# Pairing the small fp32 products of a recurrence on different rows of TensorE, with causal selects on GpSimd

## The chip, the cores and the metric

The kernel runs on one NeuronCore of a Trainium2 chip. The metric is the device time of one execution in microseconds (us). Its engines are TensorE (PE in the profile; its weight loads PEld), VectorE (DVE), ScalarE (ACT), GpSimd (POOL) and SyncE (SP, which here issues DMAs). Each works through its own instructions in program order.

## The reference, cut to what matters

A two-layer trunk over 256 positions of width 2048. Layer 0 projects its normalized input once and feeds two mixers, a gated MLP (A) and an RWKV-7 recurrence (B) with 16 heads of 64; their outputs go through one output projection. Layer 1 is attention; each layer ends in a SwiGLU FFN. The change touches only B:

```python
kk = kk / jnp.maximum(jnp.sqrt(jnp.sum(kk * kk, axis=-1, keepdims=True)), 1e-12)
...
def step(state, inp):
    r_t, w_t, k_t, v_t, a_t, b_t = inp
    sa = jnp.einsum('bhij,bhj->bhi', state, a_t)
    state = (state * w_t[:, :, None, :] + sa[..., None] * b_t[:, :, None, :]
             + v_t[..., None] * k_t[:, :, None, :])
    y_t = jnp.einsum('bhij,bhj->bhi', state, r_t)
    return state, y_t
...
y = ((y - mean) * lax.rsqrt(var + B_GN_EPS)).reshape(bsz, s, B_WIDTH)
...
y = (y + bonus.reshape(bsz, s, B_WIDTH)) * g.astype(f32)
```

## The kernel before, in words

The dense projections are the main stream. In `dense32` (layer 0's input projections) a chunk of 512 KB of fp32 weights is loaded by SP and multiplied in four fp32 matmuls of 128x512 (L901). Every fp32 matmul is two passes in the trace, so a chunk is eight L901 records. In `dense` (everything after) a chunk is split into a high part (L191 on ACT) and a low part (L192 on DVE) and takes twelve single-pass matmuls (L203 to L205).

The recurrence is a generator, `rk_gen`. After each chunk `pump` runs the adaLN work (an `ada` chunk of 512 KB and one DVE dot product, L117) and then lets `rk_gen` go on until a credit is spent: each `yield x` costs x, each chunk gives 1.8 to 3. So the small products stand between the chunks of the main stream in each engine's queue; inside that, the program's scheduler orders instructions by when their operands and PSUM banks come free. The small products share a pool of four PSUM banks (`msbank`).

The recurrence in chunks of 64 positions, with its lines: decay and `a` gates from two low-rank products (L511); the norm of kk, spread back over a head's 64 channels by `head_bcast` (L474, a 16-row product); the masked 64x128 products of every head (L637), whose results go to `SCN` (mask product L640 on DVE) and `SRA` (half by L643 on ACT and a mask product L644 on POOL, half by L647 on DVE); the inverse of a unit triangular matrix per head and chunk, by 32x32 transposes (L665), a chain of 31 pairs of DVE products (L672, L674), transposes back (L680, L683) and two 32x32 matmuls that merge the halves (L690, L699); then the state steps c = 0 to 3, with `x_free` (L738), L815, L831, L845, L852 and L862; the bonus and gate (`gate_bonus`, L474 on `bon`, L759); and a group norm in two parts (L779 to L798, L474 on the rows in `SRA`). Layer 0's output projection follows (`YA`, then `YB`).

Heads 2g and 2g+1 lie on rows 0 to 63 and 64 to 127 of a tile (index e). TensorE has 128 rows and 128 columns of cells; a product of 64, 32 or 16 rows uses only those rows.

## Time and profile before

| | |
|---|---|
| median of 3 runs | 2560.14 us (2558.58 to 2572.45) |
| the profiled execution's own time | 2557.72 us |
| its span (first to last instruction) | 2555.7 us, 2.0 us less |
| PE busy | 2429.3 us (95%) |
| DVE busy | 1619.6 us (63%) |
| ACT busy | 1037.1 us (41%) |
| POOL busy | 102.0 us (4%) |
| mean granted TensorE clock | 0.978 of full speed |

PE's records overlap (a matmul's record lasts longer than the distance to the next one), so PE's rate is read from the distance between starts. Times in the rows count from the start of the span. The recurrence runs from about 150 to 535 us.

### The profile page before, as it was taken

To read this page: it belongs to the slowest core of one execution; us is meant where nothing else is said; L and a number is where in the kernel's file an instruction comes from. 1 tells how busy PE (TensorE), PEld (TensorE's weight loads), DVE (VectorE), ACT (ScalarE), POOL (GpSimd) and SP (SyncE) were. 2 spreads that over 40 slices of the span, in tenths; PEclk is the share of its full clock that TensorE was granted. 3 is DMA by queue.
4 is the path that set the end of the run, shared out by engine and by line. 5 is a ranking of instruction groups with operands and counts; after the bars stand their busy time and mean duration, and the time that the engine had idled before them with its cause. 6 is when DMAs were issued, how large, how long until landed. Compare 5 with 4: busy or idle time off the path is not lost. (4 is left out here: it accounts for less than half of the span.)

```text
span 2555.7 us, 29570 instructions
## 1 busy us (share of the span) xinstructions
PE 2429.3 (95%) x10944; PEld 1860.5 (73%) x10944; DVE 1619.6 (63%) x2176; ACT 1037.1 (41%) x1423; POOL 102.0 (4%) x83
## 2 busy tenths in 40 slices
PE   4998989998999999999998999999899999999998
PEld 2443537677887777888887777778778888888886
DVE  5656794568877777654446778865776455444444
ACT  1042103347443443444445444446544444444443
POOL 0002210001000000000001001100100000000000
PEclk8998999899999999999999999999999999999999
DMA  9987776574988888755554888855587555556554
GB/s 377 417 302 242 259 245 212 177 265 146 329 317 306 317 296 310 234 205 191 193 193 146 302 292 311 300 196 206 201 318 265 188 190 189 189 190 206 191 194 151
DMA packets 166528, 623.47 MB, mean 244 GB/s; under 512 B 18560, under 2 KB 18752, under 8 KB 161392
## 3 DMA queue, kind: packets, MB, share of 16 engines
q1 hardware_dynamic: 164288, 612.74, 68.7%
q10 hardware_dynamic: 2096, 8.86, 0.9%
q8 instruction: 85, 1.39, 0.2%
q14 instruction: 59, 0.48, 0.1%
HBM read 619.39 MB, written 2.13 MB: 243 GB/s over the span
## 5 line engine op out<-in xcount | busy, mean ns | idle before, releaser
L192 DVE TENSOR_TENSOR wl<-w,wh 128x1024 fp32r<-128x1024 f32 x688 | 836.8, 1223 | 532.9 <-ACT wh L191 531.7
L191 ACT ACTIVATE wh<-w 128x1024 fp32r<-128x1024 f32 x688 | 728.3, 1059 | 1005.4 <-PE mm L205 941.7
L117 DVE SCALAR_TENSOR_TENSOR ada<-ada,cond 128x1024 f32<-128x1024 f32 x320 | 392.9, 1229 | 286.1 <-DMA ada<-in_w_ada_dram 285.2
L204 PE MATMUL mm<-wl,hF 128*128 128x512 f32 x1408 | 552.4, 392 | 15.0 <-DVE wl L192 14.8
L203 PE MATMUL mm<-wh,hF 128*128 128x512 f32 x1408 | 552.9, 393 | 0.0
L205 PE MATMUL mm<-wh,hFl 128*128 128x512 f32 x1408 | 549.9, 391 | 0.0
L204 PEld LDWEIGHTS mm<-wl,hF 128*128 128x128 f32 x1408 | 264.5, 188 | 81.8 <-DVE wl L192 28.6
L205 PEld LDWEIGHTS mm<-wh,hFl 128*128 128x128 f32 x1408 | 264.4, 188 | 54.5
L203 PEld LDWEIGHTS mm<-wh,hF 128*128 128x128 f32 x1408 | 264.5, 188 | 53.7
L204 PE MATMUL mm<-wl,aH 128*128 128x512 f32 x704 | 276.9, 393 | 0.0
L205 PE MATMUL mm<-wh,aL 128*128 128x512 f32 x704 | 275.5, 391 | 0.0
L203 PE MATMUL mm<-wh,aH 128*128 128x512 f32 x704 | 274.6, 390 | 0.0
L901 PE MATMUL mm<-w,xT 128*128 128x512 f32 x448 | 216.3, 630 | 4.6 <-DMA w<-in_w_in_dram 4.6
L901 PEld LDWEIGHTS mm<-w,xT 128*128 128x128 f32 x448 | 86.2, 201 | 105.9 <-issue 97.7
L203 PE MATMUL mm<-wh,hA 128*128 128x512 f32 x384 | 155.7, 405 | 0.0
L204 PE MATMUL mm<-wl,hA 128*128 128x512 f32 x384 | 152.3, 397 | 3.1 <-DVE wl L192 3.1
L203 PEld LDWEIGHTS mm<-wh,aH 128*128 128x128 f32 x704 | 132.2, 188 | 30.1
L204 PEld LDWEIGHTS mm<-wl,aH 128*128 128x128 f32 x704 | 132.3, 188 | 28.6
L205 PEld LDWEIGHTS mm<-wh,aL 128*128 128x128 f32 x704 | 132.3, 188 | 27.7
L205 PE MATMUL mm<-wh,hAl 128*128 128x512 f32 x384 | 150.8, 393 | 0.0
L204 PEld LDWEIGHTS mm<-wl,hA 128*128 128x128 f32 x384 | 72.8, 190 | 20.1 <-DVE wl L192 6.3
L205 PEld LDWEIGHTS mm<-wh,hAl 128*128 128x128 f32 x384 | 72.7, 189 | 15.1
(312 smaller groups left out, 2049.5 us busy)
## 6 DMA issues: line engine op xcount, KB each, us to landing
w<-in_w_ffn_in_dram SPq DMA_DIRECT2D x352, 512.0 KB, 3.9
ada<-in_w_ada_dram SPq DMA_DIRECT2D x320, 512.0 KB, 5.1
w<-in_w_ffn_out_dram SPq DMA_DIRECT2D x176, 512.0 KB, 3.6
w<-in_w_qkv_dram SPq DMA_DIRECT2D x96, 512.0 KB, 5.2
w<-in_w_in_dram SPq DMA_DIRECT2D x56, 512.0 KB, 5.2
w<-in_w_out_dram SPq DMA_DIRECT2D x32, 512.0 KB, 3.8
w<-in_w_o_dram SPq DMA_DIRECT2D x32, 512.0 KB, 3.3
KB<-in_w_ada_dram SPq DMA_DIRECT2D x12, 1024.0 KB, 12.0
```

Source lines behind the costliest of these rows:

```text
L117: V.scalar_tensor_tensor(w, w, 1.0, cond[:, k0:k0 + n], op0=OP.mult, op1=OP.mult, accum_out=dst)
L191: A.activation(wh[:, :, :ncol], w32[:, :, :ncol], AF.Copy)
L192: V.tensor_sub(wl[:, :, :ncol], w32[:, :, :ncol], wh[:, :, :ncol].bitcast(F32))
L203: T.matmul(o, h, wh[:, k, :ncol], start=(kt == 0), stop=False)
L204: T.matmul(o, h, wl[:, k, :ncol], start=False, stop=False)
L205: T.matmul(o, l, wh[:, k, :ncol], start=False, stop=(kt == nkt - 1))
L901: T.matmul(ps[t], xT[:, kt, tsl(t)], w[:, k, :], start=(kt == 0), stop=(kt == KT - 1))
```

## The change

Products that use 64, 32 or 16 rows are issued alternately on two groups of rows, each into a PSUM bank of its own: the two low-rank products (now 64 rows each instead of one 128-row product against zeros), `head_bcast` (a copy of the 16 rows is kept on rows 32 to 47, `twice`), the masked products over e, the merge of block b with the second half of the merge of block b-2, the state products over e, and L831 with the next chunk's `x_free`. `SRA` is evicted by ACT alone and masked by eight `affine_select` on POOL. The yields change from 8x0.7 to 4x1.0 (low-rank products), from 16x0.5 to 8x1.0 (masked products) and from 8x0.6 to 6x1.0 (merges).

```diff
-    indT = x0i[0:16, :].rearrange("h (g p) -> h g p", g=8)
+    indT = [x0i[32 * q:32 * q + 16, :].rearrange("h (g p) -> h g p", g=8) for q in range(2)]
...
-    A.dma_start(indT, io["indT"])
-
-    def head_bcast(out, g, rows):
-
-        T.matmul(out, indT[:, g, :], rows, start=True, stop=True)
+    for q in range(2):
+        A.dma_start(indT[q], io["indT"])
+
+    def twice(rows):
+
+        A.activation(rows[32:48], rows[0:16], AF.Copy)
+
+    def head_bcast(g0, n, rows):
+
+
+        w = rows.free_size()
+        ps = [msbank()[:, :n // 2 * w].rearrange("p (g s) -> p g s", g=n // 2) for _ in range(2)]
+        for i in range(n // 2):
+            for q in range(2):
+                T.matmul(ps[q][:, i, :], indT[q][:, g0 + 2 * i + q, :], rows[32 * q:32 * q + 16],
+                         start=True, stop=True)
+        return ps
...
-        for which, dst, bias in ((0, E[:, 0], "w0"), (1, AT, "a0")):
-            for g2 in range(4):
-                ps = msbank()
-                psv = ps.rearrange("p (g s) -> p g s", g=2)
+        for g2 in range(4):
+            psv = [msbank().rearrange("p (g s) -> p g s", g=2) for _ in range(2)]
+            for i in range(2):
+                g = 2 * g2 + i
+                for x in range(2):
+                    xs = slice(64 * x, 64 * x + 64)
+                    T.matmul(psv[x][:, i, :], w2a2[xs, g * P:(g + 1) * P], tz[xs],
+                             start=True, stop=True)
+            for x, dst, bias in ((0, E[:, 0], "w0"), (1, AT, "a0")):
                 for i in range(2):
                     g = 2 * g2 + i
-                    T.matmul(psv[:, i, :], w2a2[:, g * P:(g + 1) * P], tz[:, which, :],
-                             start=True, stop=True)
-                for i in range(2):
-                    g = 2 * g2 + i
-                    A.activation(dst[:, g, :], psv[:, i, :], AF.Sigmoid, bias=col(bias, g))
-                yield 0.7
+                    A.activation(dst[:, g, :], psv[x][:, i, :], AF.Sigmoid, bias=col(bias, g))
+            yield 1.0
...
+        rn2 = SCf[0:48, 0:S]
+        rn = rn2[0:16]
         A.activation(rn, pn[:16, :S], AF.Sqrt)
         V.tensor_scalar(rn, rn, 1e-12, None, op0=OP.max)
         V.reciprocal(rn, rn)
+        twice(rn2)
         yield 2.3
-        for g2 in range(4):
-            ps = msbank()
-            psv = ps.rearrange("p (g s) -> p g s", g=2)
-            for i in range(2):
-                head_bcast(psv[:, i, :], 2 * g2 + i, rn)
-            V.tensor_mul(Kk[:, 2 * g2:2 * g2 + 2, :], Kk[:, 2 * g2:2 * g2 + 2, :], psv)
-            yield 0.6
+        for g0 in (0, 4):
+            ps = head_bcast(g0, 4, rn2)
+            for q in range(2):
+                gs = slice(g0 + q, g0 + 4, 2)
+                V.tensor_mul(Kk[:, gs, :], Kk[:, gs, :], ps[q])
+            yield 1.2
...
-        ne = 0
         for c in range(4):
             cs = slice(c * 64, (c + 1) * 64)
-            for e in range(2):
-                es = slice(64 * e, 64 * e + 64)
-                for hf in range(2):
-                    ps = msbank()
-                    psv = ps.rearrange("p (g x t) -> p g x t", g=4, x=2)
-                    for i in range(4):
-                        g = 4 * hf + i
-                        T.matmul(psv[:, i], KB[es, g, c].rearrange("p b t -> p (b t)"),
+            for hf in range(2):
+                ps = [msbank().rearrange("p (g x t) -> p g x t", g=4, x=2) for _ in range(2)]
+                for i in range(4):
+                    g = 4 * hf + i
+                    for e in range(2):
+                        es = slice(64 * e, 64 * e + 64)
+                        T.matmul(ps[e][:, i], KB[es, g, c].rearrange("p b t -> p (b t)"),
                                  RA[es, :, g, cs], start=True, stop=True)
-                    gs = slice(4 * hf, 4 * hf + 4)
-                    V.tensor_tensor(SCv[:, c, gs, e, :], psv[:, :, 1, :],
+                gs = slice(4 * hf, 4 * hf + 4)
+                for e in range(2):
+                    V.tensor_tensor(SCv[:, c, gs, e, :], ps[e][:, :, 1, :],
                                     mk[:, 1:2, :].to_broadcast([P, 4, 64]), op=OP.mult)
-                    if ne % 2 == 0:
-                        A.activation(SRv[:, c, gs, e, :], psv[:, :, 0, :], AF.Copy)
-                        G.tensor_tensor(SRv[:, c, gs, e, :], SRv[:, c, gs, e, :],
-                                        mk[:, 0:1, :].to_broadcast([P, 4, 64]), op=OP.mult)
-                    else:
-                        V.tensor_tensor(SRv[:, c, gs, e, :], psv[:, :, 0, :],
-                                        mk[:, 0:1, :].to_broadcast([P, 4, 64]), op=OP.mult)
-                    ne += 1
-                    yield 0.5
+                    A.activation(SRv[:, c, gs, e, :], ps[e][:, :, 0, :], AF.Copy)
+                yield 1.0
+            for x in range(2):
+                sr = SRA[64 * x:64 * x + 64, 16 * c:16 * c + 16, :]
+                G.affine_select(sr, sr, pattern=[[0, 16], [1, 64]], compare_op=OP.is_ge, fill=0.0,
+                                base=0, channel_multiplier=-1)
...
-        for b in range(4):
-            ps = msbank()
+        def merge_ops(b, second, ps):
             for i in range(16):
                 n = 16 * b + i
-                T.matmul(ps[96:128, i * 32:(i + 1) * 32], SCN[64:96, n, 32:64], T0[64:96, n, :],
-                         start=True, stop=True)
-            A.activation(T0[96:128, 16 * b:16 * b + 16, :],
-                         ps[96:128, :].rearrange("p (n j) -> p n j", n=16), AF.Copy)
-            yield 0.6
...
+                if second:
+                    yield (ps[64:96, i * 32:(i + 1) * 32], T0[96:128, n, :], SCN[96:128, n, 32:64])
+                else:
+                    yield (ps[96:128, i * 32:(i + 1) * 32], SCN[64:96, n, 32:64], T0[64:96, n, :])
+
+        for st in range(6):
+            job = [(b, x) for b, x in ((st, 0), (st - 2, 1)) if 0 <= b < 4]
+            banks = [msbank() for _ in job]
+            for ops in zip(*(merge_ops(b, x, ps) for (b, x), ps in zip(job, banks))):
+                for o, l, r in ops:
+                    T.matmul(o, l, r, start=True, stop=True)
+            for (b, x), ps in zip(job, banks):
+                dst, o = (SCN[64:96, 16 * b:16 * b + 16, 32:64], 64) if x else (
+                    T0[96:128, 16 * b:16 * b + 16, :], 96)
+                A.activation(dst, ps[o:o + 32, :].rearrange("p (n j) -> p n j", n=16), AF.Copy)
+            yield 1.0
...
-        def x_free(c):
-            px = [msbank() for _ in range(2)]
+        def x_free(c, px):
             for e in range(2):
                 for g in range(8):
                     h = 2 * g + e
-                    T.matmul(px[e][64:128, g * 64:(g + 1) * 64], SCN[0:64, c * 16 + h, :],
-                             VU2[0:64, c % 2, h, :], start=(g == 0), stop=(c == 0 and g == 7))
-            return px
+                    yield (px[e][64:128, g * 64:(g + 1) * 64], SCN[0:64, c * 16 + h, :],
+                           VU2[0:64, c % 2, h, :], g == 0, c == 0 and g == 7)
+
+        def mm_list(ops):
+            for o, l, r, st, sp in ops:
+                T.matmul(o, l, r, start=st, stop=sp)
...
-            pb = msbank()
-            pbv = pb.rearrange("p (g s) -> p g s", g=2)
-            for i in range(2):
-                head_bcast(pbv[:, i, :], 2 * g2 + i, bon)
-            V.tensor_tensor(VT[:, gs, :], VT[:, gs, :], pbv, op=OP.mult)
+            for q, pb in enumerate(head_bcast(2 * g2, 2, bon)):
+                g = 2 * g2 + q
+                V.tensor_tensor(VT[:, g:g + 1, :], VT[:, g:g + 1, :], pb, op=OP.mult)
...
-            for e in range(2):
-                es = slice(64 * e, 64 * e + 64)
-                if c:
-                    for g in range(8):
+            if c:
+                for g in range(8):
+                    for e in range(2):
+                        es = slice(64 * e, 64 * e + 64)
                         T.matmul(px[e][64:128, g * 64:(g + 1) * 64], RA[es, 1, g, cs],
                                  Sst[es, g, :], start=False, stop=(g == 7))
+            for e in range(2):
...
+            pu = [msbank() for _ in range(2)]
+            if c < 3:
+                px = [msbank() for _ in range(2)]
+                nx = x_free(c + 1, px)
             for b in range(2):
-                ps = msbank()
                 for i in range(8):
                     h = 8 * b + i
-                    T.matmul(ps[64:128, i * 64:(i + 1) * 64], SCN[64:128, c * 16 + h, :],
+                    T.matmul(pu[b][64:128, i * 64:(i + 1) * 64], SCN[64:128, c * 16 + h, :],
                              X0[64:128, h, :], start=True, stop=True)
+                    if c < 3:
+                        mm_list([next(nx)])
                 A.activation(VU[64:128, 8 * b:8 * b + 8, :],
-                             ps[64:128, :].rearrange("p (h i) -> p h i", h=8), AF.Copy)
-            if c < 3:
-                px = x_free(c + 1)
```

Three places on PE show what moves. First the merge of the triangular blocks (`AT` and `SCN` are its operands, L690 its first product, L699 its second; L901 is a main-stream chunk). Before:

```order
L901 MATMUL mm<-w_1444,xT 128x512 x4
L690 MATMUL ms<-AT,SCN 32x32 x48
L901 MATMUL mm<-w_1507,xT 128x512 x4
L690 MATMUL ms<-AT,SCN 32x32 x16
L699 MATMUL ms<-SCN,AT 32x32 x32
```

Now (L709 is both products, L917 the chunk):

```order
L917 MATMUL mm<-w_1437,xT 128x512 x4
L709 MATMUL ms<-AT,SCN 32x32 x32
L917 MATMUL mm<-w_1482,xT 128x512 x4
L709 MATMUL ms<-AT,SCN 32x32
L709 MATMUL ms<-SCN,AT 32x32
```

The third block's first products, which stood ahead of a chunk, stand behind it and alternate with second products. Next the state step c = 1 (L831 is the inverse times X0, L738 is `x_free` of the next chunk). Before:

```order
L831 MATMUL ms<-x0i,SCN 64x64 x8
L901 MATMUL mm<-w_1873,xT 128x512
L831 MATMUL ms<-x0i,SCN 64x64 x8
L738 MATMUL ms<-AT,SCN 64x64 x4
L901 MATMUL mm<-w_1873,xT 128x512
L738 MATMUL ms<-AT,SCN 64x64 x12
```

Now (L847 and L753):

```order
L847 MATMUL ms<-x0i,SCN 64x64 x8
L917 MATMUL mm<-w_1875,xT 128x512
L753 MATMUL ms<-AT,SCN 64x64 x4
L847 MATMUL ms<-x0i,SCN 64x64 x8
L917 MATMUL mm<-w_1875,xT 128x512
L753 MATMUL ms<-AT,SCN 64x64 x12
```

Here the two products are not alternated; four `x_free` products moved ahead of the second eight. Last the bonus (L474, now L484) and the gate (L759, now L770). Before:

```order
L474 MATMUL ms<-bon,x0i 128x256 x2
L759 MATMUL ms<-sg,SRA 128x256 x4
L901 MATMUL mm<-w_2111,xT 128x512 x3
L474 MATMUL ms<-bon,x0i 128x256 x2
L759 MATMUL ms<-sg,SRA 128x256 x4
```

Now:

```order
L484 MATMUL ms<-bon,x0i 128x256 x2
L917 MATMUL mm<-w_2115,xT 128x512
L770 MATMUL ms<-sg,SRA 128x256 x4
L917 MATMUL mm<-w_2115,xT 128x512
L484 MATMUL ms<-bon,x0i 128x256
L917 MATMUL mm<-w_2178,xT 128x512
L484 MATMUL ms<-bon,x0i 128x256
L917 MATMUL mm<-w_2178,xT 128x512
```

Only the first pair of bonus products stands together; the two of each later pair are parted by a chunk's matmul.

## Rows read from the trace of the kernel before

**Rows 1.** The page: busy time of each engine, and the granted TensorE clock in 40 equal slices of the span (tenths).

```profile
PE 2429.3 (95%) x10944; PEld 1860.5 (73%) x10944; DVE 1619.6 (63%) x2176; ACT 1037.1 (41%) x1423; POOL 102.0 (4%) x83
...
PEclk8998999899999999999999999999999999999999
```

**Rows 2.** Busy time by stretch: stretch and its length, then PE, PEld, DVE, ACT, POOL busy (instructions), granted clock, share of DMA, GB/s.

```profile
140.00:302.65 162.65, 152.97 (x480) 74.20 (x479) 104.28 (x207) 51.14 (x96) 28.17 (x29) 0.96 0.77 262
302.65:387.15 84.50, 70.74 (x240) 34.43 (x239) 77.48 (x133) 8.15 (x14) 15.11 (x8) 0.91 0.69 230
387.15:541.00 153.85, 153.48 (x1293) 106.47 (x1294) 89.17 (x153) 56.87 (x91) 0.00 (x0) 0.93 0.63 209
468.00:485.00 17.00, 17.00 (x32) 7.47 (x32) 7.44 (x13) 4.33 (x8) 0.00 (x0) 0.50 0.39 125
```

**Rows 3.** Timeline of PE: start, length, line, shape, count; the low-rank products, a chunk, and `head_bcast` of the kk norm.

```profile
158.47 2.75 PE L511 MATMUL ms<-tz,w2a 128*128 128x256 f32 x12
161.06 3.60 PE L901 MATMUL mm<-w,xT 128*128 128x512 f32 x8
...
212.48 2.85 PE L474 MATMUL ms<-SCN,x0i 16*128 16x256 f32 x12
...
220.59 1.12 PE L474 MATMUL ms<-SCN,x0i 16*128 16x256 f32 x4
```

**Rows 4.** Timeline of PE: the masked products among the chunks (in brackets idle time before, and who ended it).

```profile
279.79 1.16 PE L637 MATMUL ms<-RA,KB 64*128 64x128 f32 x8
280.88 3.70 PE L901 MATMUL mm<-w,xT 128*128 128x512 f32 x8
284.51 3.16 PE L637 MATMUL ms<-RA,KB 64*128 64x128 f32 x32
...
291.23 1.16 PE L637 MATMUL ms<-RA,KB 64*128 64x128 f32 x8
293.31 2.60 PE L637 MATMUL ms<-RA,KB 64*128 64x128 f32 x24 [0.92 <-ACT SRA L643]
295.84 3.70 PE L901 MATMUL mm<-w,xT 128*128 128x512 f32 x8
...
308.82 3.65 PE L637 MATMUL ms<-RA,KB 64*128 64x128 f32 x32
```

**Rows 5.** Timeline of PE, state step c = 2: where L831 (rows 64 to 127) meets L738 (rows 0 to 63).

```profile
447.69 0.22 PE L738 MATMUL ms<-AT,SCN 64*64 64x64 f32 x1
447.69 0.22 PE L831 MATMUL ms<-x0i,SCN 64*64 64x64 f32 x1
447.75 1.85 PE L738 MATMUL ms<-AT,SCN 64*64 64x64 f32 x29
449.53 1.13 PE L901 MATMUL mm<-w,xT 128*128 128x512 f32 x2
```

**Rows 6.** DVE by line and shape: the two mask products (busy us, mean ns).

```profile
L640 DVE TENSOR_TENSOR SCN<-ms,cst 128x256 f32<-128x256 f32 x16 | 6.4, 417 | 0.0
...
L647 DVE TENSOR_TENSOR SRA<-ms,cst 128x256 f32<-128x256 f32 x8 | 3.3, 414 | 0.0
```

**Rows 7.** Timeline of DVE: the first transposes, and three products of the triangular chain.

```profile
302.65 3.89 DVE L665 STREAM_TRANSPOSE AT<-SCN 32x1024 f32<-32x1024 f32 x2
...
361.96 2.48 DVE L672 TENSOR_TENSOR AT<-AT,KBn 128x175 f32<-128x175 f32 x1
...
366.88 0.32 DVE L672 TENSOR_TENSOR AT<-AT,KBn 128x156 f32<-128x156 f32 x1
```

**Rows 8.** Timeline of POOL: the one `affine_select` there is, and the two products after the inner LayerNorm.

```profile
178.91 1.09 POOL L918 TENSOR_SCALAR_AFFINE_SELECT wsT<-wsT 128x1024 f32<-128x1024 f32 x1 [43.58 <-DMA wsT<-in_wsT_dram]
...
360.04 6.61 POOL L942 TENSOR_TENSOR vA<-vA,gn 128x1024 f32<-128x1024 f32 x2 [41.50 <-DVE vA L941]
```

**Rows 9.** Timeline of PE: the merges.

```profile
381.52 3.59 PE L690 MATMUL ms<-AT,SCN 32*32 32x32 f32 x64 [7.11 <-DVE AT L683]
387.27 1.89 PE L690 MATMUL ms<-AT,SCN 32*32 32x32 f32 x32 [2.15 <-DVE AT L683]
389.08 5.55 PE L901 MATMUL mm<-w,xT 128*128 128x512 f32 x8
394.56 1.10 PE L690 MATMUL ms<-AT,SCN 32*32 32x32 f32 x29
...
395.59 2.09 PE L699 MATMUL ms<-SCN,AT 32*32 32x32 f32 x61
...
403.03 2.21 PE L699 MATMUL ms<-SCN,AT 32*32 32x32 f32 x64
```

**Rows 10.** Timeline of PE: one state product over both e, and the first bonus products.

```profile
423.48 1.90 PE L815 MATMUL ms<-Sst,RA 64*64 64x64 f32 x32
...
456.31 1.13 PE L474 MATMUL ms<-bon,x0i 16*128 16x256 f32 x4
```

**Rows 11.** Timeline of all engines: one step of the group norm on DVE and ACT, and its `head_bcast` products on PE.

```profile
490.74 0.56 DVE L780 TENSOR_TENSOR RA<-RA,ms 128x384 f32<-128x384 f32 x1 [0.99 <-PE ms L779]
...
491.33 0.52 ACT L781 ACTIVATE KB<-RA 128x384 f32<-128x384 f32 x1 [2.79 <-DVE RA L780]
...
512.84 1.56 PE L474 MATMUL ms<-SRA,x0i 16*128 16x192 f32 x8
...
521.17 1.99 PE L474 MATMUL ms<-SRA,x0i 16*128 16x64 f32 x16
```

More of the change, by code (lines that the diff above doesn't have):

```diff
@@ L608, in rk_gen @@
             yield 0.7
-        A.activation(bon, pb[:16, :S], AF.Copy)
+        A.activation(bon[0:16], pb[:16, :S], AF.Copy)
+        twice(bon)
         for g in range(8):
@@ L685, in rk_gen @@
             yield 1.1
-        for b in range(4):
-            ps = msbank()
+        def merge_ops(b, second, ps):
             for i in range(16):
                 n = 16 * b + i
-                T.matmul(ps[96:128, i * 32:(i + 1) * 32], SCN[64:96, n, 32:64], T0[64:96, n, :],
-                         start=True, stop=True)
-            A.activation(T0[96:128, 16 * b:16 * b + 16, :],
-                         ps[96:128, :].rearrange("p (n j) -> p n j", n=16), AF.Copy)
-            yield 0.6
-        for b in range(4):
-            ps = msbank()
-            for i in range(16):
-                n = 16 * b + i
-                T.matmul(ps[64:96, i * 32:(i + 1) * 32], T0[96:128, n, :], SCN[96:128, n, 32:64],
-                         start=True, stop=True)
-            A.activation(SCN[64:96, 16 * b:16 * b + 16, 32:64],
-                         ps[64:96, :].rearrange("p (n j) -> p n j", n=16), AF.Copy)
-            yield 0.6
+                if second:
[13 more added lines that the diff above has]
+            yield 1.0
         dump("TT", SCN)
@@ L785, in group_norm @@
                 yield 0.6
-            rv = rvt[0:16, 0:n]
+            rv2 = rvt[0:48, 0:n]
+            rv = rv2[0:16]
             A.activation(rv, pv_[:16, :n], AF.Sqrt, bias=eps_g[:16], scale=1.0 / 64)
             V.reciprocal(rv, rv)
+            twice(rv2)
             yield 1.5
@@ L791, in group_norm @@
                 gs = slice(g0, g0 + gw)
-                pr_ = msbank()
-                prv = pr_[:, :gw * n].rearrange("p (g s) -> p g s", g=gw)
-                for i in range(gw):
-                    head_bcast(prv[:, i, :], g0 + i, rv)
-                V.tensor_tensor(Y[:, gs, ts], Y[:, gs, ts], prv, op=OP.mult)
+                for q, prv in enumerate(head_bcast(g0, gw, rv2)):
+                    gq = slice(g0 + q, g0 + gw, 2)
+                    V.tensor_tensor(Y[:, gq, ts], Y[:, gq, ts], prv, op=OP.mult)
                 V.tensor_tensor(Y[:, gs, ts], Y[:, gs, ts], GT[:, gs, ts], op=OP.mult)
@@ L805, in rk_gen @@
         yield 1.0
-        px = x_free(0)
+        px = [msbank() for _ in range(2)]
+        mm_list(x_free(0, px))
         for c in range(4):
@@ L826, in rk_gen @@
                     yield next(gn01)
+            pu = [msbank() for _ in range(2)]
+            if c < 3:
+                px = [msbank() for _ in range(2)]
+                nx = x_free(c + 1, px)
             for b in range(2):
-                ps = msbank()
                 for i in range(8):
                     h = 8 * b + i
-                    T.matmul(ps[64:128, i * 64:(i + 1) * 64], SCN[64:128, c * 16 + h, :],
+                    T.matmul(pu[b][64:128, i * 64:(i + 1) * 64], SCN[64:128, c * 16 + h, :],
                              X0[64:128, h, :], start=True, stop=True)
+                    if c < 3:
+                        mm_list([next(nx)])
                 A.activation(VU[64:128, 8 * b:8 * b + 8, :],
-                             ps[64:128, :].rearrange("p (h i) -> p h i", h=8), AF.Copy)
-            if c < 3:
-                px = x_free(c + 1)
+                             pu[b][64:128, :].rearrange("p (h i) -> p h i", h=8), AF.Copy)
             yield 1.0
```

10 lines of the change are left out of this document (4 added, 6 removed).

## The prediction

> **What bounds the kernel now.** I read the page first: PE is busy 95% of the span and no other engine is above 63% [rows 1]. That share is an average, so the next view is the busy time in the stretch where the recurrence runs, cut where the bound changes [rows 2]. From 140 to 302.65 us PE is busy 152.97 of 162.65 us and DVE 104.28: PE sets the pace there (stretch A). From 302.65 to 387.15 DVE is busy 77.48 of 84.50 us and PE 70.74: the triangular chain and the ada dot products fill DVE, and PE waits for them at the end (B). From 387.15 to 541 PE is busy 153.48 of 153.85 us and DVE 89.17 (C). So a nanosecond taken off PE is worth its full length in A and C, and nothing in B; one taken off DVE is worth its length only in B. Outside this stretch the diff changes nothing.
>
> B begins when DVE can start the first transposes [rows 7], which need the masked products of c = 0 and 1; it ends when the last transposes let PE go on: PE stood 7.11 us before the merges and 2.15 us inside them, released by DVE both times [rows 9].
>
> **Does pairing work here?** The kernel before issues its products one row group at a time, but where L831 and L738 meet, the trace has both: records of the two lines start at the same 447.69, and the next at 447.75; then 29 records of L738 alone take 1.78 us to the next line, 0.061 us each [rows 5]. Two row groups thus pass two records in the time of one. I take half the time per record for every product that is really alternated.
>
> A visit to a narrow product also has a fixed price. Eight records of L637 take 1.16 us and 32 take 3.65 us [rows 4]: 0.104 us a record and 0.33 us a visit, of which 0.07 is the overlap of the last record; I take 0.26. The chunk behind such a visit lasts 3.70 us [rows 4] instead of 3.60 behind the low-rank products, which use all 128 rows [rows 3]: 0.10 more. A visit costs 0.36 us whether the products in it are paired or not.
>
> **Stretch A.** Low-rank products: 12 records take 2.59 us from their start to the chunk behind [rows 3], 0.216 each, 32 records 6.9 us. Paired, 3.45; but as 64-row products they now pay for three visits, 1.1 us. Saved 2.4 us (at least 0 if they don't overlap at all, less 1.1).
> `head_bcast` of the kk norm: 12 records 2.85 and 4 records 1.12 us [rows 3], 0.216 a record, 3.97 in two visits. As eight pairs in one visit 8 x 0.216 + 0.26 = 1.99. Saved 2.0. The copy `twice` adds to ACT lies under the main-stream chunk that stands between; uncovered it would cost one small ACT instruction, about the 0.52 us of a 384-wide one at most [rows 11].
> Masked products: B waits for the first 64 records. Before, the first 72 took 1.16 + 3.16 + 4.61 us (the last from 291.23 to 295.84, with a wait of 0.92 for a bank) [rows 4], 8.9, less 0.8 for the eight too many: 8.1. Now 64 x 0.052 + 3 x 0.26 = 4.1. Saved 4.0. The other half lies in B, hidden by DVE.
> The yields of the low-rank products fall from 5.6 to 4.0, at 1.8 a chunk about one chunk. B then begins a chunk earlier and C has a chunk more: this moves time, it makes none. A: 8.4 us.
>
> **Stretch B.** Eight mask products of 0.41 us leave DVE [rows 6]; four of them lie in B, 1.6 us, and one `SCN` mask product (0.42) comes into it, since the transposes come sooner. Against that stand the selects on POOL. The only one in the trace takes 1.09 us [rows 8]. Two DVE products took 2.48 us and its like, where 0.32 is usual for such a size [rows 7], while POOL's two products from 360.04 on were running [rows 8]: one engine held up the other. Four selects in B can cost DVE between 0 (POOL waits) and 4.4 us; POOL's old mask products leave at the same time. I take 1.2. B: 0.
>
> **Stretch C.** Merges: from 381.52 to the chunk at 389.08 they took 7.56, then 1.10, 2.09 and 2.21 us [rows 9], 12.96. In the new order the first 64 records cost 3.59 as before; then PE has a chunk to run while DVE finishes, so the 2.15 us wait is covered; the other 192 records alternate at half of 2.09/61, 3.3 us, and three visits 0.8. That is 7.7, saved 5.3; part of it will run at the low clock, as 381 to 389 did (96 records in 3.59 + 1.89 us [rows 9]): I take 4.5. The Trainium skill (TensorEngine Tiling (Array Packing), Instruction Overhead) says that a matmul costs some 60 cycles however few columns it has, so that tiling gains nothing on a dimension that is already small; by that the 192 records would take an estimated 4.8 us, and 1.5 of the 4.5 would be gone. No row here shows paired 32-column products for long enough to decide it.
> State products over e (L815): three visits of 1.90 us [rows 10]; paired 32 x 0.0305 + 0.26 = 1.24. Saved 2.0.
> L831 with `x_free`: the order keeps them in separate runs, with only eight pairs made in all; a pair saves two records of 0.061 [rows 5] less what the meeting points saved already. 0.3, of the 4 or so that full pairing would give.
> Bonus: the first pair saves 0.43, but three pairs are parted by chunks, three visits more: loss 0.7. One visit cost 1.13 before [rows 10].
> Group norm: 1.56 twice and 1.99 us [rows 11]; paired 0.91, 0.91, 1.13. Saved 2.2, of which I take 1.5, because DVE must take the results as before and now in twice as many pieces. In the new order its first part stands without chunks between its steps, so one step of DVE and ACT, 0.56 + 0.52 us [rows 11], comes to light: loss 1.1.
> C: 4.5 + 2.0 + 0.3 - 0.7 + 1.5 - 1.1 = 6.5 us.
>
> **Sum.** 8.4 + 0 + 6.5 = 14.9 us off 2557.72, the profiled execution's own time (its span and 2.0 us around it): 2542.8. The median of the runs shown is 2.4 us above that execution, so 2545.2; I say 2545.
>
> **The rivals.** (1) The clock comes back. From 468 to 485 PE was busy without a gap, yet the granted clock was 0.50, the lower level, after the bonus and gate products; 17 us at half rate cost 8.5 [rows 2]. The bonus products now stand between chunks. If that stretch stays at the full clock, 14.9 + 8.5 = 23.4 saved: 2537. The records say only what ran before the fall, not what would prevent it.
> (2) POOL holds DVE. If every select blocks DVE, 8 x 1.09 = 8.7 us, half of it in B, and the merges' gain is smaller by 1.5: 14.9 - 3.2 - 1.5 = 10 saved, 2550. For it: the long L672 [rows 7]. Against: DVE's mask products were never longer than usual beside POOL's (mean 0.417 [rows 6]). The Trainium skill (SBUF — State Buffer, SBUF: two separate sides) says that a DVE instruction with two SBUF inputs and a GpSimd one that reads SBUF exclude each other for a whole instruction; the L672 row agrees.
> (3) The saved PE time turns into waits: the chain through DVE and ACT, not PE's rate, sets A, and two banks at once make PE wait for evictions as it did at 293.31 [rows 4]. Then A gives about half, 4, and C 4: 8 saved, 2552.
> (4) Slower: the low clock spreads. Pairs use few columns and are over sooner, and PE's work in C is mostly these. 17 us cost 8.5; to eat up 14.9 and the 12.8 of half a percent, 55 us more of C at 0.50 are needed, to lose the gain alone 30. Against it: C as a whole had 0.93 [rows 2]. At 60 us: 2575. That no product overlaps at all, only the order changes, would give some 3 us of gain at most, 2557.
>
> **How the numbers follow.** Half a percent, 12.8 us, is about what a measurement of this kernel can tell from no change; it lies at 2547.3. The forecast has 0.50, with a range of its own of 2540 to 2550, so 0.07 of it falls short of that line. (1) 0.14; (2) 0.13; (3), with the case of no overlap, 0.15; (4) 0.08. Faster 0.43 + 0.14 = 0.57; same 0.07 + 0.13 + 0.15 = 0.35; slower 0.08. The range leaves out 2 in 10: below it takes in most of (1), with all of the upper bounds 2531; above it goes to no gain, 2560.
>
> **What would show it.** Right: paired lines with two records per 0.06 us (state) and 0.11 us (masked); the first transposes some 8 us and a chunk earlier; no wait inside the merges, a chunk between their first 64 records and the rest; L847 and L753 still in separate runs. Wrong: L672-like records over 1 us beside the selects; a granted clock below 0.9 from the merges to the group norm; a longer wait of PE at the masked products or at the group norm.

## The result, and the profile after

| | before | after |
|---|---|---|
| median (10 runs each) | 2561.04 us | 2546.84 us (2540.51 to 2554.62) |
| ratio | | 0.9946, 95% interval 0.9927 to 0.9964 |
| profiled span | 2555.7 us | 2542.5 us |

The kernel became 0.54% faster; the forecast was 2545 us. The ten runs lie in two groups, 2540.5 to 2544.3 and 2549.4 to 2554.6 us, so a few us between two medians say little by themselves. The page of after, its busy times and the granted clock, answers to [rows 1]:

```profile
PE 2411.9 (95%) x10944; PEld 1841.5 (72%) x10944; DVE 1614.1 (63%) x2176; ACT 1037.0 (41%) x1433; POOL 105.5 (4%) x82
...
PEclk8999999999999999999999999999999999999999
```

The busy times by stretch, cut as [rows 2] at the first transposes and the first merges of this run (columns as there):

```profile
140.00:301.39 161.39, 143.09 (x472) 66.55 (x472) 101.65 (x200) 49.59 (x101) 30.98 (x29) 0.95 0.77 256
301.39:376.80 75.41, 65.93 (x183) 29.61 (x180) 66.91 (x128) 8.28 (x16) 15.02 (x9) 0.95 0.77 259
376.80:541.00 164.20, 157.61 (x1390) 107.22 (x1391) 102.17 (x174) 61.65 (x99) 1.24 (x1) 0.94 0.66 223
468.00:485.00 17.00, 17.00 (x74) 8.15 (x74) 8.73 (x20) 7.16 (x15) 0.00 (x0) 0.80 0.54 182
```

In the first stretch PE is now busy 143.09 of 161.39 us, where it was busy 152.97 of 162.65: 9.9 us less (3.6 of it the chunk that has gone to a later stretch), but it stands idle for 18.3 us instead of 9.7. From 468 to 485 the granted clock is 0.80 instead of 0.50. Where the waits are, in PE's timeline (idle time before and its releaser in brackets; L522 low-rank, L584 and L617 the two 16-row sums over a head, L484 `head_bcast`, L649 masked products):

```profile
154.84 1.14 PE L522 MATMUL ms<-tz,w2a 64*128 64x256 f32 x8
155.91 3.70 PE L917 MATMUL mm<-w,xT 128*128 128x512 f32 x8
159.54 2.00 PE L522 MATMUL ms<-tz,w2a 64*128 64x256 f32 x16
161.46 3.70 PE L917 MATMUL mm<-w,xT 128*128 128x512 f32 x8
...
193.92 1.89 PE L584 MATMUL ms<-sq,cst 128*16 128x256 f32 x4 [8.21 <-ACT sq L583]
...
211.11 2.16 PE L484 MATMUL ms<-SCN,x0i 16*128 16x256 f32 x16
...
247.29 0.60 PE L617 MATMUL ms<-q,cst 128*16 128x256 f32 x2 [2.75 <-DVE q L615]
...
252.41 0.60 PE L617 MATMUL ms<-q,cst 128*16 128x256 f32 x2 [3.46 <-DVE q L615]
...
284.05 1.16 PE L649 MATMUL ms<-RA,KB 64*128 64x128 f32 x16
...
293.34 2.00 PE L649 MATMUL ms<-RA,KB 64*128 64x128 f32 x16 [2.67 <-ACT SRA L655]
295.27 4.82 PE L917 MATMUL mm<-w,xT 128*128 128x512 f32 x8
...
302.00 3.70 PE L917 MATMUL mm<-w,xT 128*128 128x512 f32 x8
```

The pairs themselves run as forecast: eight low-rank records take 1.07 us to the chunk's start and sixteen 1.92, so four pairs more cost 0.85, 0.21 a pair, as one record did in [rows 3]; the sixteen of `head_bcast` take 2.1 us instead of 3.97. But PE arrives early and stands: 8.21 us at L584 and 6.2 at L617 in the two rows.

To see the whole I add up, for each line, the distances between PE's starts, with PE's idle time put down to the line that ends it, and which part of the former lay at the lower clock (by the clock at each start). Between the same two records of the main stream, one just ahead of the recurrence (146.65 us before, 147.22 after) and one in the output projection behind it (581.78 and 569.40):

| | before | after |
|---|---|---|
| between the two records | 435.14 | 422.18 |
| of it PE working | 407.67 | 387.80 |
| (of that at the lower clock) | 49.6 | 36.9 |
| of it PE waiting | 27.46 | 34.38 |

Of the 19.9 us of work less, 6.3 are clock (12.7 us less at half rate), 13.5 are work; 6.9 went into waits. Cut by the main stream's own progress (29 and 46 of its 56 chunks done), the three stages took 149.2, 75.0 and 211.0 us before and 154.8, 78.3 and 189.1 after. The first two became longer and the third 21.9 shorter; the recurrence now stands a chunk earlier in them, so some of its work lies in an earlier stage.

### The profile page after: what moved, and what is told of

It reads as the page before. It is cut to its first block, busy times and chain, and to the rows that moved or that the text cites. A ratio compares the mean times of both kernels' runs of the same rounds, so it can differ in the third digit from the quotient of the medians.

```text
span 2542.5 us, 29576 instructions
## 1 busy us (share of the span) xinstructions
PE 2411.9 (95%) x10944; PEld 1841.5 (72%) x10944; DVE 1614.1 (63%) x2176; ACT 1037.0 (41%) x1433; POOL 105.5 (4%) x82
## 5 line engine op out<-in xcount | busy, mean ns | idle before, releaser
L117 DVE SCALAR_TENSOR_TENSOR ada<-ada,cond 128x1024 f32<-128x1024 f32 x320 | 396.2, 1239 | 289.2 <-DMA ada<-in_w_ada_dram 287.8
L917 PE MATMUL mm<-w,xT 128*128 128x512 f32 x448 | 216.5, 630 | 4.2 <-DMA w<-in_w_in_dram 4.1
L917 PEld LDWEIGHTS mm<-w,xT 128*128 128x128 f32 x448 | 85.3, 199 | 105.4 <-issue 97.2
L203 PEld LDWEIGHTS mm<-wh,aH 128*128 128x128 f32 x704 | 132.1, 188 | 29.5
```

Source lines behind the costliest of these rows:

```text
L117: V.scalar_tensor_tensor(w, w, 1.0, cond[:, k0:k0 + n], op0=OP.mult, op1=OP.mult, accum_out=dst)
L203: T.matmul(o, h, wh[:, k, :ncol], start=(kt == 0), stop=False)
L917: T.matmul(ps[t], xT[:, kt, tsl(t)], w[:, k, :], start=(kt == 0), stop=(kt == KT - 1))
```

## The experiments

Twelve kernels, each beside runs of the kernel before on the same chip. Ratios are against those; times are medians. Four of the first eight undo one part of the change.

**u_unpaired.** The order of issue alone; here the masked products, and the same swap in every loop that alternates:

```diff
-                for i in range(4):
-                    g = 4 * hf + i
-                    for e in range(2):
+                for e in range(2):
+                    for i in range(4):
+                        g = 4 * hf + i
                         es = slice(64 * e, 64 * e + 64)
                         T.matmul(ps[e][:, i], ...)
```

> The changed kernel in all but one thing: in every loop that alternates two groups of rows, the products of the one group are issued first and those of the other behind them, into the same banks, with the same credits. On PE nothing else moves: chunks and visits stand where they stood. Theory (overlap): what the change saves on PE is two row groups working at once, so the lines get slower again by what the accounting of PE's starts gives between before and after: low-rank 2.9, kk norm and group norm 3.6, masked products 3.4, merges 2.7, state products over e 1.7, L847 with L753 0.9, together 15 us; some of it fills waits of PE (12 us in the first half), so the time is 2555 to 2562. Rival (order): the gain comes from where the products stand and from the clock, not from overlap: the lines keep their times and the whole stays within 3 us of 2547.

Measured: 2548.08 us (five runs, 2540.2 to 2549.7), 0.9948 (0.9923 to 0.9972), which can't be told from the changed kernel's 0.9946. So the overlap theory failed in its time. A part of the reason stands in its timeline of PE, in the low-rank, the masked and the state products, unpaired:

```profile
159.21 2.10 PE L522 MATMUL ms<-tz,w2a 64*128 64x256 f32 x16
...
288.50 2.82 PE L649 MATMUL ms<-RA,KB 64*128 64x128 f32 x32
...
419.01 1.90 PE L827 MATMUL ms<-Sst,RA 64*64 64x64 f32 x32
```

In the changed kernel the same three take 2.00 (above), 2.06 and 1.15 us:

```profile
300.01 2.06 PE L649 MATMUL ms<-RA,KB 64*128 64x128 f32 x32
...
420.13 1.15 PE L827 MATMUL ms<-Sst,RA 64*64 64x64 f32 x32
```

Low-rank products, two of a group at a time (four records), overlap as well without alternation; runs of four products (eight records) in part; runs of eight only where the groups meet. What PE lost in the rest, 7.7 us at full clock, it had again elsewhere in this profile: 2.3 us less waiting, and 12 us less at the lower clock, worth 6.

**y_credits.** The credits of before:

```diff
-            yield 1.0
+            yield 1.4     # low-rank products
...
-            yield 1.0
+            yield 0.8     # merges
```

> The changed kernel with the credits of before: 4 x 1.4 = 5.6 for the low-rank products (4.0 in the change) and 6 x 0.8 = 4.8 for the merges (6.0 in the change). Theory (credits made the new waits): in the changed kernel PE waits 8.2 us at L584 and 6.7 at L617 because the recurrence was moved one chunk ahead of what DVE and the DMA can deliver; with the old credits the products stand behind one chunk more, these waits fall back to the 4.7 and 2.8 us of before, and the time is 2538 to 2542. Rival (DVE sets the pace there): the waits only move to other lines; PE's idle time in the recurrence stays at about 34 us and the time within 3 us of 2547.

Measured: 2555.72 us, 0.9980 (0.9963 to 0.9996): 9 us slower. L584's wait did fall from 8.2 to 3.8, yet PE's whole idle time rose from 34.4 to 38.8. Both theories miss the time. Part of the 9 us is the clock: over the ten runs of each the mean granted clock was 0.979 here and 0.981 in the changed kernel, an estimated 5 us of 2550. How much is left for the earlier recurrence itself, net of the wait it makes, is not shown; the profiled execution took 2561.75 us, the longest of the ten.

**b_credits**, the other way round, the kernel before with the change's credits:

```diff
-                yield 0.7
+                yield 0.5      # low-rank products, eight times
...
-            yield 0.6
+            yield 0.75     # merges, eight times
```

> The kernel before with the credits of the change: 8 x 0.5 = 4.0 for the low-rank products and 8 x 0.75 = 6.0 for the merges; nothing else. Theory (the credits carry a good part of the gain, as the changed kernel without them took 2555.7 us): the recurrence stands a chunk earlier, the merges have a chunk between their halves, the 2.15 us wait inside them goes, and the time falls by 6 to 9 us, to 2551 to 2554. Rival (the credits are worth something only together with the cheaper products, or the 9 us were the clock's): 2558 to 2562.

Measured: 2551.38 us, 0.9978 (0.9961 to 0.9996), as the theory said. The first transposes come at 292.4 us instead of 302.65, a chunk earlier and 6.7 us beyond that, without a single pair. Between the two records PE's work at full clock is that of before (383.2 us against 382.9); what is less is 14.0 us at the lower clock, worth 7.0, and 3.5 us of waiting.

**k_bonus** and **b_bonus**, the bonus products put back into one bank, and split over two banks in the kernel before:

```diff
-            for q, pb in enumerate(head_bcast(2 * g2, 2, bon)):
-                g = 2 * g2 + q
-                V.tensor_tensor(VT[:, g:g + 1, :], VT[:, g:g + 1, :], pb, op=OP.mult)
+            pb = msbank()
+            pbv = pb.rearrange("p (g s) -> p g s", g=2)
+            for i in range(2):
+                head_bcast1(pbv[:, i, :], 2 * g2 + i, bon[0:16])
+            V.tensor_tensor(VT[:, gs, :], VT[:, gs, :], pbv, op=OP.mult)
```

> The changed kernel with the bonus products as before: the two of a call in one bank, on rows 0 to 15 alone. In the order on PE they stand again in a run with the gate products, as in the kernel before. Theory (the bonus order gave back the clock): in the kernel before PE ran at the lower level for 17 us from 468 on, behind these products; in the changed kernel for 6.8 us. With the old order the 17 us return and the time is about 5 us longer, 2552. Rival (the clock there doesn't hang on the bonus): the low stretch stays at about 7 us, and the time falls by the 0.7 us that three visits less are worth, 2546.

> The kernel before with one edit: the two bonus products of a call go to a bank each, both still on rows 0 to 15, and DVE multiplies them singly. On PE chunk matmuls now stand between the bonus and the gate products, as in the changed kernel; nothing is paired and no credit is touched. Theory (the order gives back the clock): the low stretch behind the bonus products shrinks from 17 to about 7 us, the mean granted clock over the runs rises from 0.978 to about 0.980, and the time falls by 5 to 8 us, to 2552 to 2555. Rival (the clock needs the rest of the change too): the 17 us stay and the time is 2560, or 1 us more for the added visits.

Measured: k_bonus 2556.07 us, 0.9978 (0.9963 to 0.9993), 9 us slower than the change; b_bonus 2555.86, 0.9989 (0.9964 to 1.0014), some 3 us faster than before, not clear of no change. Busy times from 456 to 490 us, of k_bonus:

```profile
456.00:490.00 34.00, 34.00 (x108) 15.53 (x106) 19.31 (x36) 9.87 (x18) 0.00 (x0) 0.75 0.58 184
```

of the changed kernel:

```profile
456.00:490.00 34.00, 33.71 (x163) 17.81 (x163) 19.61 (x40) 14.25 (x26) 0.00 (x0) 0.90 0.62 210
```

and of b_bonus:

```profile
456.00:490.00 34.00, 34.00 (x162) 17.11 (x157) 24.70 (x46) 14.04 (x25) 0.00 (x0) 1.00 0.71 226
```

The column behind POOL is the granted clock, a mean of its two levels, 0.50 (1.2 GHz) and 1.00 (2.4 GHz): 0.75 with the bonus and gate products in a run, as in the kernel before, 0.90 and 1.00 with chunk matmuls between them. Over all ten runs the mean granted clock was 0.977 for k_bonus and 0.981 for the change, an estimated 10 us of 2550 and so the whole difference; PE's work at full clock is the same in both profiles (369.2 and 369.4 us). Of the fourteen profiles of this case the four with the old order (before, k_bonus, b_credits, p_only) have 0.75 to 0.80 there; of the ten with the new, nine have 0.90 or 1.00 and one, y_credits, 0.80. And m_tt, with the changed kernel's order row for row, has 1.00 where that has 0.90. So the order bears on the clock, but does not set it alone.

**m_masks**, **m_copy**, **m_tt**, on the eviction of `SRA`. m_masks restores the old masking (ACT and POOL for e = 0, DVE for e = 1); the other two change one side each:

```diff
 # m_copy
-                    A.activation(SRv[:, c, gs, e, :], ps[e][:, :, 0, :], AF.Copy)
+                    if e == 0:
+                        A.activation(SRv[:, c, gs, e, :], ps[e][:, :, 0, :], AF.Copy)
+                    else:
+                        V.tensor_copy(SRv[:, c, gs, e, :], ps[e][:, :, 0, :])
 # m_tt: the affine_select calls go, and behind each eviction by ACT
+                    G.tensor_tensor(SRv[:, c, gs, e, :], SRv[:, c, gs, e, :],
+                                    mk[:, 0:1, :].to_broadcast([P, 4, 64]), op=OP.mult)
```

> The changed kernel with SRA masked as before: e = 0 evicted by ACT and multiplied on POOL, e = 1 multiplied on DVE straight from the bank; the pairs of products stay. Theory (selects are free): the eight selects cost DVE about as much as eight mask products did; time within 2 us of 2547. Rival (selects hold DVE, ACT's evictions hold PE): in the changed kernel the dot products beside the selects took 2.08, 1.74 and 1.47 us instead of 1.23, and PE waits 5.3 us for banks that ACT evicts in turn; without them both go back, and the time is 2541 to 2544. Third: eight more products on DVE keep banks longer, PE waits more, 2550.

> The changed kernel with one edit: SRA's e = 1 half is copied out of its bank by DVE instead of ACT; the selects on POOL stay. It parts the two sides of the run with the old masks, which took 2540. Theory (ACT's serial evictions held PE): with the copies spread over ACT and DVE PE's waits at the masked products fall from 5.3 to about 2.8 us and the time is 2540 to 2543. Rival (the selects held DVE): the dot products beside the selects still take 1.5 to 2.1 us, and the time stays at 2546 to 2549.

> The changed kernel with one edit: ACT still evicts all of SRA, but POOL masks it with sixteen products against the mask, as the kernel before did for half of it, instead of eight selects. Theory (ACT's serial evictions held PE): they are still there, so PE's waits at the masked products stay at about 5 us and the time at 2546 to 2549. Rival (the selects held DVE): the products on POOL take 0.7 to 1.7 us each but don't lengthen the dot products, and the time falls to 2540 to 2543.

Measured: m_masks 2539.99 us, 0.9921 (0.9900 to 0.9943); m_copy 2539.72, 0.9928 (0.9902 to 0.9954); m_tt 2545.61, 0.9948 (0.9928 to 0.9968). By the medians the selects are free: m_copy keeps them and has the whole gain, m_tt drops them and has none. (m_masks and m_copy have four and five runs, and the intervals of all three overlap.) By the expectations that makes ACT's evictions the cause. The order of PE's instructions points elsewhere. That of m_tt is, row for row, the changed kernel's; that of m_copy is, row for row, m_masks', and it differs from the changed kernel's behind the merges alone. Around the bonus, the changed kernel (L917 a chunk matmul, L484 bonus, L770 gate, L827 state, L790 and L794 group norm):

```
L484 MATMUL ms<-bon,x0i 128x256 x2
L917 MATMUL mm<-w_2115,xT 128x512
L770 MATMUL ms<-sg,SRA 128x256 x4
...
L484 MATMUL ms<-bon,x0i 128x256
L770 MATMUL ms<-sg,SRA 128x256 x4
...
L794 MATMUL ms<-KB,cst 16x192 x2
L790 MATMUL ms<-RA,cst 128x384 x3
```

and m_copy (where the lines behind L484 have numbers three higher):

```
L484 MATMUL ms<-bon,x0i 128x256
L920 MATMUL mm<-w_2115,xT 128x512
L484 MATMUL ms<-bon,x0i 128x256
L920 MATMUL mm<-w_2115,xT 128x512
L773 MATMUL ms<-sg,SRA 128x256 x4
...
L797 MATMUL ms<-KB,cst 16x192 x2
L793 MATMUL ms<-RA,cst 128x384 x2
L920 MATMUL mm<-w_2227,xT 128x512
```

m_copy has two chunk matmuls more between these small products. Its clock there (its bonus begins earlier, at 444.84 us, so the stretch holds a later part of it):

```profile
456.00:490.00 34.00, 33.84 (x242) 21.04 (x242) 25.19 (x53) 16.46 (x29) 0.00 (x0) 1.00 0.63 199
```

1.00 instead of 0.90. By main-stream progress the third stage takes 189.1 us in the change and 191.4 in m_tt, but 181.8 in m_copy and 183.5 in m_masks. Between the two records m_copy is 10.9 us shorter than the change: 7.3 of it lie in that stage, behind the merges, and 1.8 at the masked products, where it waits 3.5 us instead of 5.3. Moving work from ACT to DVE changed what the scheduler did more than 100 us later. That this order makes the time is likely, but not shown. PE's work at full clock is no less (369.6 us against 369.4); m_copy's 10.9 us are 7.9 of clock and 3.2 of waits, while m_masks, with the same order, has 2.6 of clock and 7.2 of waits. And over all runs the mean granted clock hardly differs (0.981 and 0.982, against 0.981).

**m_copy_u**, m_copy with the unpaired order of u_unpaired (both diffs above):

> The run that took 2539.7 (SRA's e = 1 half copied by DVE) with the unpaired order of issue in all loops. Undoing the alternation cost the changed kernel only 1 us. Theory (PE's saved time sank into waits and the clock, overlap itself is worth some 8 us): with the masked products' waits gone, more of it shows, and the time is 2543 to 2548. Rival (short runs overlap anyway and the rest is too small to see): 2538 to 2542.

Measured: 2548.22 us, 0.9953 (0.9927 to 0.9979). The number is the theory's, the reading isn't: without the alternation the scheduler put the products behind the merges back among the chunk matmuls as in the changed kernel, and the time is that kernel's. Like u_unpaired it shows unpaired products at one order of the rest, and again the cost, about 1 us, can't be told from none. Its order on PE is that of u_unpaired row for row, and so is its time within 0.2 us, though DVE evicts half of `SRA` in the one and ACT all of it in the other. That speaks for the order too, with one limit: without the alternation PE waits only 2.6 us at the masked products in either, so there is less for the evictions to hold.

**a_ada** and **m_copy_ada**, a lower rate of the adaLN dot products in the first half, alone and with m_copy:

```diff
         while "lora" not in have:
             yield None
+        Ada.rate = 0.6
```

> The changed kernel with one edit: from its first step until the first transposes the recurrence sets the rate of the adaLN dot products to 0.6 per chunk instead of 1.0, so about 16 of them (and their 512 KB loads) are done later. Theory (DVE works in order: the recurrence's products stand behind dot products that wait for their loads, 53.7 us of waiting in the first half, and PE waits for those products): PE's waits at L584 and L617, 8.2 and 6.7 us, fall below half, and the time to 2539 to 2543. Rival (ACT and the credits set these waits): the waits stay above 12 us together and the time at 2546 to 2549. Third: the dot products come back where DVE sets the pace, the triangular chain, 16 x 1.23 us later, and the time is 2550 or more.

> Both edits on the changed kernel, the candidate for a faster version: SRA's e = 1 half copied by DVE, adaLN at 0.6 per chunk in the first half. If the two causes add: 2532 to 2536. If either alone frees the same wait: 2538 to 2541.

Measured: a_ada 2539.23 us, 0.9932 (0.9904 to 0.9960); m_copy_ada 2532.30, 0.9904 (0.9876 to 0.9932), the fastest kernel here, below the change by 14 us of medians or 11 by the ratios (its ten runs took 2530.7 to 2550.1). The time came, the mechanism didn't: the dot products (L117) from 140 to 302 us, then from 385 to 600 us, of the changed kernel

```profile
L117 DVE SCALAR_TENSOR_TENSOR ada<-ada,cond x48: 1198/1225/2084, 141.2 to 299.9; 128x1024 f32<-128x1024 f32 x48
...
L117 DVE SCALAR_TENSOR_TENSOR ada<-ada,cond x41: 1214/1224/1227, 388.2 to 553.0; 128x1024 f32<-128x1024 f32 x41
```

and of a_ada

```profile
L117 DVE SCALAR_TENSOR_TENSOR ada<-ada,cond x47: 1203/1226/2137, 141.9 to 296.6; 128x1024 f32<-128x1024 f32 x47
...
L117 DVE SCALAR_TENSOR_TENSOR ada<-ada,cond x30: 1215/1225/1227, 384.9 to 491.9; 128x1024 f32<-128x1024 f32 x30
```

The first half kept its dot products, and L584 and L617 together still waited 11.6 us (5.0 and 6.6). Eleven left the last stage. Of the 10.6 us that this kernel is shorter between the two records, 8.2 are clock and 2.2 waits; PE's work at full clock is the same. The theory on DVE's order was therefore not tested by this run.

**p_only**, the pairs alone: the changed kernel with the edits of y_credits, k_bonus and m_masks.

> The pairs alone: the changed kernel with the credits of before (4 x 1.4, 6 x 0.8), the bonus products in one bank on one row group as before, and SRA masked as before (ACT and POOL for e = 0, DVE for e = 1). What is left of the change is the alternated products of the low-rank step, the kk and group norms, the masks, the merges, the state and L847 with L753. Theory (overlap is worth the 8.5 us that undoing it cost beside the DVE copies, and the parts add): 2560 - 8.5 or somewhat more, for the merges now have a chunk between their halves: 2548 to 2552. Rival (the saved time needs the other credits to show): 2556 to 2561.

Measured: 2559.15 us, 0.9986 (0.9967 to 1.0006; the kernel before had a median of 2564.0 beside it). The rival holds: the pairs by themselves bring 3.6 us by the ratio, which is not clear of none. In its profile PE works 13.9 us less than in the kernel before and waits 13.4 us more.

## Why the prediction was right

The number was right, and that it was so close is luck: the way to it was right in most of its parts and wrong in what they add up to. The terms, from the same addition by line, at full clock (time at the lower clock counted half):

| term | forecast | measured |
|---|---|---|
| low-rank | -2.4 | -2.9 |
| `head_bcast` of kk | -2.0 | -1.8 |
| masked products | -4.0 in the first half | -3.9 in both halves |
| merges, products | -4.5 with the wait inside | -1.7, and waits 9.27 to 3.33 |
| state products over e | -2.0 | -2.3 |
| L831 and `x_free` | -0.3 | -0.9 |
| bonus, visits | +0.7 | +0.2 |
| group norm | -1.5 | -1.6 |
| a step of the group norm uncovered | +1.1 | no wait there |
| waits at L584, L617 and the masked products | 0 | +10.6 |
| chunks between them, and the rest | in the terms | +1.4, and waits +2.2 |
| lower clock | 0 | -6.3 |

**Pairing costs half.** Right, at every line that is alternated. Also right: a chunk between the first 64 records of the merges and the rest, no wait inside them, L847 and L753 mostly in separate runs, bonus pairs parted. The merges, of the changed kernel (PE's timeline, the third stage where two blocks alternate):

```profile
376.80 3.59 PE L709 MATMUL ms<-AT,SCN 32*32 32x32 f32 x64 [3.33 <-DVE AT L693]
380.31 6.66 PE L917 MATMUL mm<-w,xT 128*128 128x512 f32 x8
386.90 0.21 PE L709 MATMUL ms<-AT,SCN 32*32 32x32 f32 x1
386.91 0.21 PE L709 MATMUL ms<-SCN,AT 32*32 32x32 f32 x1
386.95 0.19 PE L709 MATMUL ms<-AT,SCN 32*32 32x32 f32 x1
386.96 0.19 PE L709 MATMUL ms<-SCN,AT 32*32 32x32 f32 x1
...
388.03 3.70 PE L917 MATMUL mm<-w,xT 128*128 128x512 f32 x8
```

64 records in the 1.13 us to the next chunk, two every 0.03 us, where [rows 9] has one. The Trainium skill's sentence that a matmul costs some 60 cycles however few columns it has (TensorEngine Tiling (Array Packing), Instruction Overhead) would have made them an estimated 1.6 us; the measurement decides: the cost is not added up over two row groups. I counted 192 records as alternated; the last two stages of the six stand alone, so only 128 are.

**Stretch A: the step that failed.** "A: 8.4 us" took PE to set the pace there, because it was busy 152.97 of 162.65 us [rows 2]. It did so only as long as it was slow. The first transposes come at 301.39 us, with one chunk less done before them but only 1.3 us earlier, where the chunk alone is some 3.6: without it the way there became 2 us longer instead of 8 shorter. The products were cheaper, but what they wait for is made by DVE and ACT at their own times: PE's 4.72, 2.78 and 2.18 us of waiting at L572, L604 and L637 became 8.21, 6.74 and 5.29. p_only shows it with the credits, bonus order and masks of before: 13.9 us less work, 13.4 more waiting. That is the mechanism of rival (3), which I gave 0.15 with the case of no overlap. The waits stood in the trace of before, and I counted only the one of 0.92 us. A longer wait at the masked products was one of my own signs of being wrong, and it came.

**Stretch B.** Forecast 0. The transposes-to-merges time fell by 3.5 us (78.87 to 75.41), with 17 chunks in it both times. The selects lengthened dot products, though not by much. DVE and POOL in the changed kernel:

```profile
293.69 3.22 POOL L659 TENSOR_SCALAR_AFFINE_SELECT SRA<-SRA 64x1024 f32<-64x1024 f32 x2 [29.67 <-ACT SRA L655]
293.82 2.08 DVE L117 SCALAR_TENSOR_TENSOR ada<-ada,cond 128x1024 f32<-128x1024 f32 x1
...
299.14 3.22 POOL L659 TENSOR_SCALAR_AFFINE_SELECT SRA<-SRA 64x1024 f32<-64x1024 f32 x2 [2.23 <-ACT SRA L655]
299.87 1.47 DVE L117 SCALAR_TENSOR_TENSOR ada<-ada,cond 128x1024 f32<-128x1024 f32 x1 [1.22 <-DMA ada<-in_w_ada_dram]
```

2.08 and 1.47 us, and 1.74 for one between them, instead of 1.23: 1.6 us in all, near the 1.2 that I took. Rival (2) is out as a bound: m_copy keeps the selects. What the forecast of 0 missed is POOL's four products after the inner LayerNorm. Before, four products of the triangular chain stood beside them and took 2.27 to 2.48 us, where the others take at most 0.43: the one of [rows 7], the next one (2.37 us) and

```profile
370.48 2.37 DVE L672 TENSOR_TENSOR AT<-AT,KBn 128x60 f32<-128x60 f32 x1
372.88 2.27 DVE L674 TENSOR_TENSOR KBn<-KBn,AT 128x60 f32<-128x60 f32 x1
```

In the changed kernel they fall beside one product of the chain and one dot product, and beside transposes, which keep their length:

```profile
363.57 5.18 POOL L958 TENSOR_TENSOR vA<-vA,gn 128x1024 f32<-128x1024 f32 x2 [42.07 <-issue]
364.26 2.28 DVE L684 TENSOR_TENSOR KBn<-KBn,AT 128x87 f32<-128x87 f32 x1
366.46 3.37 DVE L117 SCALAR_TENSOR_TENSOR ada<-ada,cond 128x1024 f32<-128x1024 f32 x1
...
373.37 4.67 POOL L963 TENSOR_TENSOR vA<-vA,bi 128x1024 f32<-128x1024 f32 x2 [4.62 <-DMA bi<-in_a_v_bias_dram]
```

The 62 products of the chain take 23.1 us instead of 29.5, the dot products 2.2 more. I had read the long one in the trace of before, but took it to stay. So the shorter wait in front of the merges (7.11 to 3.33 us) goes with this change of place, and not with the pairs.

**Stretch C.** Forecast 6.5 us; merges to the output projection's record fell from 200.3 to 192.6 although a chunk more stands there, so some 11. The difference is the clock: 17 us at the lower level behind the bonus products became 7, as rival (1) put it, and k_bonus brought them back (3.4 and 13.7 us) and lost 8 to 9 us. I had it at 0.14 because no record said what would prevent the fall.

**The sum.** 14.9 us forecast for pairs and covered waits; 13.5 of work were saved, 6.9 of it lost in waits and 6.3 given back by the clock. Two rivals came true at once and cancelled. One thing held in every profile: PE's work at full clock between the two records is 368 to 370 us in the nine kernels with alternated products, whatever else they changed, 376 to 377 in the two unpaired ones, and 383 to 384 without the change's products. So the pairs do save the work; what tells the kernels apart is how much of it waits (27 to 41 us) and the lower clock (20 to 49 us) give back. What the whole hangs on is neither of the two things in the change's words: the pairs alone (p_only) bring 3.6 us or none, taking the alternation off the change costs about 1 us or none (u_unpaired), and the selects bring nothing; the credits alone bring 5.6 us by the ratio, the bonus order alone 2.8, which is not clear of none. These parts don't add: taken off the change one at a time, credits and bonus order cost 8 to 9 us each, together more than the whole gain.

**What stays open.** Why L584 and L617 wait longer. L584 needs both the pairs and the new credits: its wait is 3.8 us with the pairs and the old credits (y_credits, p_only) and 4.9 with the credits alone (b_credits). L617's grows with the pairs alone (6.7 and 5.6 us in the same two, against 2.9). That DVE stands behind dot products whose load is late (53.7 us of such waiting in stretch A) fits, but a_ada left those where they were. Why fewer dot products behind the merges, or another order there, are worth 7 us: in the profiles it is clock and waits, and no run parts them. And for u_unpaired how much of the missing 7.7 us the clock gave: its one profile says 6, while the mean clock over five runs (0.982, against 0.981 of the change) can't tell.

## What to carry to other kernels

An engine that is 95% busy in a stretch is the bound there only until it is a little faster: before counting its saved time, read who releases each of its waits in that stretch, and let the saving end where the next releaser does. Where a scheduler decides the order, compare the order of two variants before giving their difference in time a cause: here three pairs of kernels with one order each had one time each within 1.3 us, whatever their edits. And split a change that does four things at once into its parts in both directions, since here the parts did not add.

## What was not expected of the hardware

TensorE overlaps products on different row groups without alternation, as long as each group's run is short: runs of two products cost 2.10 us for sixteen records against 2.00 alternated, runs of four 2.82 for thirty-two against 2.06 (3.65 before, [rows 4], in runs of eight), and runs of eight of the state product 1.90 against 1.15. So most of the low-rank gain came with the 64-row halves, not with the alternation. Two 32-row products of 32 columns pass every 0.03 us together. And the granted clock from 456 to 490 us was 0.75 to 0.80 in the four kernels whose 16-row bonus products stood in a run with the gate products, with PE busy for all of the 34 us, and 0.90 to 1.00 in nine of ten where 512-column chunk matmuls stood between them, with PE busy for 32.8 to 34.0.
